# Gate and up products of a hybrid encoder's FFNs as 2x2 block products with seven half-size products

## The chip, the cores and the metric

The kernel runs on one core of a Trainium2 chip. The metric is the device time of one execution in microseconds; lower is better. TensorE multiplies matrices, VectorE (DVE in the profile) and ScalarE (ACT) do element-wise work and read and write PSUM, GpSimd (POOL) helps with element-wise work on SBUF, and SyncE (SP) starts the loads. Each engine runs its own instructions in order and waits on semaphores for the others.

## The reference

Two layers work on 512 tokens of 1024 features in float32. Every layer is a half-step SwiGLU FFN, a mixer (a Conformer convolution in layer 0, a bidirectional HGRN2 recurrence in layer 1) and a second half-step FFN; there are four FFNs in all.

```
def swiglu(h, w13, w2):
    gate, up = jnp.split(h @ w13, 2, axis=-1)
    return (jax.nn.silu(gate) * up) @ w2

for layer in range(DEPTH):
    x = x + FFN_RES * swiglu(rms_norm(x, norm_g[layer, 0]), ffn_w13[layer, 0], ffn_w2[layer, 0])
    h = rms_norm(x, norm_g[layer, 1])
    mix = conformer_conv(...) if layer % 2 == 0 else hgrn2_bidirectional(...)
    x = x + mix
    x = x + FFN_RES * swiglu(rms_norm(x, norm_g[layer, 2]), ffn_w13[layer, 1], ffn_w2[layer, 1])
return rms_norm(x, final_g)
```

The product `h @ w13` takes 1024 features to 2 x 2816 (gate and up); `w2` takes 2816 back to 1024.

## The kernel before

Activations lie with features on the 128 partitions: `xs[k]`, k = 0 to 7, are eight tiles of 128 features by 512 tokens. The norm's gain is applied and each tile is split into a rounded part and a rest, `xh[k]` (cast on ScalarE, L230) and `xl[k]` (VectorE, L231), in the format fp32r. Weights are split in the same way after they are loaded: ScalarE casts `whi` (L124), VectorE subtracts to get `wlo` (L125). A product of full accuracy is then three matmuls:

```
    def mm3(o, wh, wl, ah, al, first, last):
        nc.tensor.matmul(o, lhsT=wh, rhs=ah, start=first, stop=False)
        nc.tensor.matmul(o, lhsT=wh, rhs=al, start=False, stop=False)
        nc.tensor.matmul(o, lhsT=wl, rhs=ah, start=False, stop=last)
```

An FFN (L340) runs in two halves of 11 pairs. A pair j is one tile of 128 gate features and the same tile of up features; each is a `proj` (L306) of 8 k-tiles x 3 matmuls of 512 columns (one column per token), so a pair is 48 matmuls. Its evacuation (L357 to L365) multiplies both by the norm's factor `rs` (L358, L360), takes the SiLU (L362), multiplies (L363) and splits the result into `gh`, `gl` (L364, L365). After the 11 pairs of a half come 8 output tiles o of the down product, 33 matmuls each, added to `xs[o]` (L399). In the second half every finished `xs[o]` is at once prepared for the next phase (`next_prep`, L400 to L401): the split above, and its squares added up on GpSimd (L241).

The RMS norm's factor is not ready when a phase's first products start. `Lead` (L277) puts the small products of the norm between the first groups and holds evacuations back until the factor is there. In an FFN the factor is worked out in every partition at once (`norm_wide`, L258: two matmuls and some ten VectorE instructions of 512 columns); before the convolution and the recurrence it is worked out on 4 columns (`norm_stats_pe`, L243) and spread by four small products (`norm_bc`, L252).

The convolution and the recurrence end with a D-to-D product (`k_outer`): six output tiles are accumulated side by side and finish one after another (six matmuls each at the end), then output tiles 6 and 7 follow with 24 matmuls each, whose weights come from one last chunk in two parts. Each finished tile updates `xs[o]` (L634 or L925) and goes through `next_prep`.

A static scheduler orders each engine's instructions at build time and sets the semaphores; `whi`/`wlo` rotate through three buffers, raw weights through three, and PSUM has six banks for products (tag `mm`) and two for small ones (`aux`).

## Time and profile before

| | |
|---|---|
| time, median of 3 runs | 2073.39 us (2072.43 to 2074.63) |
| profiled execution: span from first to last instruction | 2068.9 us (the page gives no time around it) |
| TensorE busy | 2029.7 us, 98% of the span, 9223 matmuls |
| VectorE busy | 1111.9 us, 54% |
| ScalarE busy | 766.5 us, 37% |
| mean granted TensorE clock | 0.993 of full speed |

The span is 4.5 us below the median of the timed runs. Busy times are the union of an engine's instructions. TensorE's instructions overlap in the records: a matmul is listed with its whole duration, and the next one starts before it is over, so the rate is read from the distance of two starts. PEld is the load of the stationary operand, which each matmul has.

### The profile page before, as it was taken

The page shows a single profiled execution, that of the slowest core. Times are in us where ns is not written, and L with a number is a line of the kernel's source. Part 1 is how long each engine was busy: PE and PEld are TensorE (multiplying, and loading weights), DVE is VectorE, ACT ScalarE, POOL GpSimd, SP SyncE. Part 2 cuts the span into 40 slices and gives each one's busy share as a digit, 9 for nine tenths or more (in the row PEclk, how much of TensorE's full clock was granted, in tenths as well). Part 3 has the DMA queues.
Part 4 walks back from the last instruction along what each step waited for, and adds up shares of the span by engine and source line. Part 5 has one row for each costly group of instructions (what it writes and reads, how often), then busy time and mean ns, then how long its engine had stood idle before and what let it go on. Part 6 is the DMA issues. An engine that isn't in the chain of part 4 may idle for free.

```text
span 2068.9 us, 22882 instructions
## 1 busy us (share of the span) xinstructions
PE 2029.7 (98%) x9223; PEld 1656.7 (80%) x9223; DVE 1111.9 (54%) x1560; ACT 766.5 (37%) x1151; POOL 254.4 (12%) x201
## 2 busy tenths in 40 slices
PE   8999999998899999999999999999999999999997
PEld 6888888765688888888888888888888888888886
DVE  7433444598674434445443444378758865434433
ACT  5322233566343222233222323355545443222332
POOL 2000001399420000010000001111101020000002
PEclk9999999999899999999999999999999999999998
DMA  5223223211122232223223222311111122223221
GB/s 196 96 71 129 90 75 111 82 56 46 57 100 87 84 110 102 83 91 122 84 82 111 101 83 91 121 62 61 62 62 52 51 102 102 77 97 108 90 84 55
DMA packets 32170, 182.49 MB, mean 88 GB/s; under 512 B 3536, under 2 KB 6736, under 8 KB 17088
## 3 DMA queue, kind: packets, MB, share of 16 engines
q1 hardware_dynamic: 31376, 180.04, 25.0%
q8 instruction: 72, 1.18, 0.2%
q10 hardware_dynamic: 544, 0.52, 0.1%
q0 software_dynamic: 144, 0.46, 0.1%
q14 instruction: 34, 0.28, 0.0%
HBM read 178.92 MB, written 2.10 MB: 87 GB/s over the span
## 4 chain that ended last, share of the span: by engine, by line
PE 88%; DVE 6%; POOL 3%; issue 2%; ACT 1%; DMA 0%; SPq 0%; DVEq 0%; POOLq 0%
PE mm L153 27%; PE mm L151 27%; PE mm L152 27%; PE aux L778 2%; POOL ga L507 2%; DVE mm L499 1%; DVE wlo L125 1%; DVE Q L812 1%; PE mm L681 1%; PE mm L683 1%; PE mm L682 1%; PE aux L850 1%; DVE k L813 1%; PE mm L490 1%; PE aux L852 0%
## 5 line engine op out<-in xcount | busy, mean ns | idle before, releaser
L124 ACT CAST whi<-wraw 128x1024 fp32r<-128x1024 f32 (+3 forms) x386 | 362.3, 940 | 990.3 <-PE mm L152 710.5
L151 PE MATMUL mm<-xh,whi 128*128 128x512 f32 x1792 | 710.8, 397 | 7.5 <-ACT whi L124 7.5
L153 PE MATMUL mm<-xh,wlo 128*128 128x512 f32 x1792 | 702.0, 392 | 4.4 <-DVE wlo L125 4.3
L152 PE MATMUL mm<-xl,whi 128*128 128x512 f32 x1792 | 700.1, 391 | 0.9 <-DVE xl L231 0.9
L125 DVE TENSOR_TENSOR wlo<-wraw,whi 128x1024 fp32r<-128x1024 f32 (+3 forms) x386 | 428.5, 1111 | 242.9 <-ACT whi L124 238.7
L153 PEld LDWEIGHTS mm<-xh,wlo 128*128 128x128 f32 x1792 | 337.1, 188 | 78.2 <-DVE wlo L125 8.6
L151 PEld LDWEIGHTS mm<-xh,whi 128*128 128x128 f32 x1792 | 337.5, 188 | 76.9 <-ACT whi L124 7.5
L152 PEld LDWEIGHTS mm<-xl,whi 128*128 128x128 f32 x1792 | 337.5, 188 | 72.2 <-issue 3.4
L151 PE MATMUL mm<-gh,whi 128*128 128x512 f32 (+1 forms) x715 | 279.6, 391 | 0.0
L153 PE MATMUL mm<-gh,wlo 128*128 128x512 f32 (+1 forms) x715 | 278.5, 390 | 0.0
L152 PE MATMUL mm<-gl,whi 128*128 128x512 f32 (+1 forms) x715 | 276.4, 387 | 0.0
L241 POOL TENSOR_TENSOR ss<-ss,sq 128x512 f32<-128x512 f32 x48 | 71.3, 1485 | 1477.0 <-ACT sq L240 1469.9
L360 DVE TENSOR_TENSOR t<-mm,rs 128x512 f32<-128x512 f32 x88 | 60.8, 691 | 267.2 <-PE mm L153 267.2
L153 PEld LDWEIGHTS mm<-gh,wlo 128*128 128x128 f32 x715 | 134.2, 188 | 30.7
L152 PEld LDWEIGHTS mm<-gl,whi 128*128 128x128 f32 x715 | 134.3, 188 | 29.7
L151 PEld LDWEIGHTS mm<-gh,whi 128*128 128x128 f32 x715 | 134.4, 188 | 27.3
L358 DVE TENSOR_TENSOR t<-mm,rs 128x512 f32<-128x512 f32 x88 | 60.8, 691 | 171.7 <-PE mm L153 171.6
L399 DVE SCALAR_TENSOR_TENSOR x<-mm,x 128x512 f32<-128x512 f32 x63 | 43.6, 692 | 124.8 <-PE mm L153 124.8
L507 POOL TENSOR_TENSOR ga<-ga,pr 128x512 f32<-128x512 f32 x67 | 99.4, 1484 | 23.6 <-ACT pr L506 19.9
L364 ACT CAST gh<-t 128x512 fp32r<-128x512 f32 x88 | 54.5, 621 | 71.6 <-DVE t L363 71.6
L499 DVE SCALAR_TENSOR_TENSOR mm<-u,vec,mm 128x512 f32<-128x512 f32 x106 | 74.5, 745 | 4.3 <-PE mm L490 4.0
L778 PEld LDWEIGHTS aux<-Q,kp 128*128 128x128 f32 x448 | 58.5, 191 | 17.7 <-issue 10.0
(209 smaller groups left out, 1621.5 us busy)
## 6 DMA issues: line engine op xcount, KB each, us to landing
wraw<-in_w SPq DMA_DIRECT2D x87, 1024.0 KB, 4.8
wraw<-in_w SPq DMA_DIRECT2D x64, 704.0 KB, 4.1
wraw<-in_win SPq DMA_DIRECT2D x16, 1024.0 KB, 4.8
wraw<-in_pw SPq DMA_DIRECT2D x8, 1024.0 KB, 4.8
wraw<-in_kout SPq DMA_DIRECT2D x8, 768.0 KB, 4.2
wraw<-in_win_i SPq DMA_DIRECT2D x4, 1024.0 KB, 4.8
x<-in_xT SPq DMA_DIRECT2D x8, 256.0 KB, 5.9
wraw<-in_kout SPq DMA_DIRECT2D x2, 1024.0 KB, 4.7
```

Of the source, the lines that this page charges most:

```text
L124: nc.scalar.copy(hi[:, a:b], raw[:, off + a:off + b])
L125: nc.vector.tensor_tensor(lo[:, a:b], raw[:, off + a:off + b], hi[:, a:b].bitcast(F32), op=ALU.subtract)
L151: nc.tensor.matmul(o, lhsT=wh, rhs=ah, start=first, stop=False)
L152: nc.tensor.matmul(o, lhsT=wh, rhs=al, start=False, stop=False)
L153: nc.tensor.matmul(o, lhsT=wl, rhs=ah, start=False, stop=last)
L241: nc.gpsimd.tensor_tensor(norm["ss"], norm["ss"], sq, op=ALU.add)
L358: nc.vector.tensor_tensor(gs, pg, rs(), op=ALU.mult)
L360: nc.vector.tensor_tensor(us, pu, rs(), op=ALU.mult)
L364: nc.scalar.copy(h_, us)
L499: nc.vector.scalar_tensor_tensor(acc, u[:, t:t + S], wcol(j, t), acc, op0=ALU.mult, op1=ALU.add)
L507: nc.gpsimd.tensor_tensor(ga, ga, pr, op=ALU.add)
L778: nc.tensor.matmul(sp[:, c * P:(c + 1) * P], lhsT=kp[:, c * P:(c + 1) * P], rhs=view(Q, hl, c), start=True, stop=True)
```

## The change

The 2x2 block product splits three things in two: the output of a pair (gate tile, up tile), the features summed over (even k-tiles, odd k-tiles; the layout of `w13` puts them in four runs of 512 columns: a11, a12 for gate, a21, a22 for up) and the tokens (left 256, right 256: b11, b12 for even, b21, b22 for odd k-tiles). Instead of eight block products there are seven, of sums and differences of the blocks (Winograd's form of Strassen's product).

- Weights (`seven_w`): per pair VectorE forms four sums of 512 columns (s12 and s43), then four operands are split: wa (s12, 1024 columns), wb (a11 and a12 as loaded, 1024), wc (s43, 1024) and wd (a22, 512). The splits use the lines L129 and L130 now. wa, wb and wc together take all three `whi`/`wlo` buffers; wd has one of its own.
- Activations (`seven_x`): per two k-tiles seven operands of 256 columns (slots 0 to 6 of `x7h`, `x7l`), four of them sums or differences.
- Products (`seven`, `seven_pair`): each of the seven is 4 k-tiles x 3 matmuls of 256 columns, so 84 matmuls a pair. They are accumulated into two PSUM tiles x (gate) and y (up); ScalarE copies partial results (L468, L469, L492, L497), VectorE adds others (both through the helper `add`, L149). The seventh product, of wd, is put into the next pair (`close`). The first pair of a half has another order and a third tile z (L482, L485).
- The first two pairs of the first FFN stay plain products, on the same operand tiles (`plain_pairs`); `seven_x` of all eight tiles comes between them and rewrites slots that the second reads.
- The evacuation no longer multiplies `up` by the norm's factor; the factor, halved (`rs05`), is applied to the down product instead, which then takes two VectorE instructions per output tile (L579 and an add) in place of one.
- The FFNs use the norm on 4 columns too; `norm_wide` is gone. Before the first products six matmuls of ones run.
- The convolution's and the recurrence's `next_prep` is `seven_x` now, as is that between the third and the second FFN.

```
+NP = KD // 2
+T2 = S // 2
...
+PLAIN = 2
...
-                plan.append((w13[f, half * HALF + j], [1024, 1024]))
+                plain = f == 0 and half == 0 and j < PLAIN
+                plan.append((w13[f, half * HALF + j], [1024, 1024] if plain else [2048]))
...
+            if sz > D:
+                ready[i] = seven_w(raws[ci])
+                state["split"] += 1
+                continue
             hi = wp.tile([P, D], F32R, name="whi", tag="whi", bufs=3)
...
+    def seven_w(raw):
+        q = D // 2
+        a11, a12, a21, a22 = (raw[:, i * q:(i + 1) * q] for i in range(4))
+        s12 = st["R"].tile([P, D], F32, name="s12", tag="s12")
+        s43 = st["R"].tile([P, D], F32, name="s43", tag="s43")
+        add(s12[:, :q], a21, a22)
+        add(s12[:, q:], s12[:, :q], a11, ALU.subtract)
+        wa = wtile()
+        split(*wa, s12, 0, 0, D)
+        wb = wtile()
+        split(*wb, raw, 0, 0, D)
+        add(s43[:, :q], a12, s12[:, q:], ALU.subtract)
+        add(s43[:, q:], a11, a21, ALU.subtract)
+        wc = wtile()
+        split(*wc, s43, 0, 0, D)
+        wd = [st["R"].tile([P, q], F32R, name=n, tag=n) for n in ("wdh", "wdl")]
+        split(*wd, raw, 3 * q, 0, q)
+        return wa, wb, wc, wd
...
+    def open_x7():
+        st["R"] = r = operands("x7")
+        for n, l in (("x7h", x7h), ("x7l", x7l)):
+            l[:] = [r.tile([P, 7 * T2], F32R, name=f"{n}{k}", tag=f"{n}{k}") for k in range(NP)]
...
+    for _ in range(6):
+        nc.tensor.matmul(psum(), lhsT=ones_r, rhs=ones_r[:, 0:1].broadcast_to([P, S]), start=True, stop=True)
...
+    def seven_x(k, gc):
+        kp, g = k // 2, col(gc + k)
+        h, l = x7h[kp], x7l[kp]
+        left, right = xs[k][:, :T2], xs[k][:, T2:]
+        def both(a, b, src):
+            nc.scalar.copy(h[:, a * T2:b * T2], src)
+            add(l[:, a * T2:b * T2], src, h[:, a * T2:b * T2].bitcast(F32), ALU.subtract)
+        def less(o, a, b):
+            nc.vector.scalar_tensor_tensor(o, a, g, b, op0=ALU.mult, op1=ALU.subtract)
+        if k % 2 == 0:
+            fa = tp.tile([P, S], F32, name="t0", tag="t0")
+            fb = tp.tile([P, S], F32, name="t1", tag="t1")
+            st["f"] = fa, fb
+            nc.scalar.activation(fb[:, :T2], right, AF.Copy, scale=g)
+            nc.scalar.activation(fa[:, :T2], left, AF.Copy, scale=g)
+            add(fa[:, T2:], fb[:, :T2], fa[:, :T2], ALU.subtract)
+            both(0, 2, fa)
+        else:
+            fa, fb = st["f"]
+            fc = tp.tile([P, S], F32, name="t2", tag="t2")
+            o = slice(2 * T2, 4 * T2)
+            nc.scalar.activation(h[:, o], xs[k], AF.Copy, scale=g)
+            less(l[:, o], xs[k], h[:, o].bitcast(F32))
+            less(fc[:, :T2], right, fb[:, :T2])
+            less(fc[:, T2:], right, fa[:, T2:])
+            both(4, 6, fc)
+            less(fb[:, T2:], left, fc[:, T2:])
+            both(6, 7, fb[:, T2:])
...
+        for n, f in (("rs", 1.0), ("rs05", 0.5)):
+            norm[n] = tp.tile([P, S], F32, name=n, tag=n, bufs=1)
+            nc.scalar.mul(norm[n], b, f)
...
+    def plain_x(k, b12):
+        kp = k // 2
+        if k % 2:
+            o = slice(2 * T2, 4 * T2)
+            return [(slice(0, S), x7h[kp][:, o], x7l[kp][:, o])]
+        o = slice(kp % 2 * T2, (kp % 2 + 1) * T2)
+        return [(slice(0, T2), x7h[kp][:, :T2], x7l[kp][:, :T2]),
+                (slice(T2, S), b12[kp // 2][0][:, o], b12[kp // 2][1][:, o])]
...
+                wnext()
+                for k in range(KD):
+                    seven_x(k, C_NORM)
...
+    def seven(o, w, i, slot, start=False, kps=range(NP)):
+        x = slice(slot * T2, (slot + 1) * T2)
+        for kp in kps:
+            sl = slice((i * NP + kp) * P, (i * NP + kp + 1) * P)
+            for a, b in ((w[0], x7h), (w[0], x7l), (w[1], x7h)):
+                nc.tensor.matmul(o, lhsT=a[:, sl], rhs=b[kp][:, x], start=start and kp == 0 and a is w[0] and b is x7h,
+                                 stop=kp == NP - 1 and a is w[1], skip_group_check=True)
+    def seven_pair(lead, close, done):
+        wa, wb, wc, wd = wget()
+        x, y = psum(), psum()
+        l, r = slice(0, T2), slice(T2, S)
+        cs = st["R"].tile([P, 3 * T2], F32, name="cs", tag="cs")
+        p5, u2, u3 = (cs[:, i * T2:(i + 1) * T2] for i in range(3))
+        def seed():
+            nc.scalar.copy(y[:, l], x[:, l])
+            nc.scalar.copy(p5, x[:, r])
+        if close is None:
+            z = psum()
+            for kps in (range(NP - 1), range(NP - 1, NP)):
+                seven(x[:, r], wa, 0, 1, True, kps)
+                seven(x[:, l], wb, 0, 0, False, kps)
+                if kps[-1] == NP - 1:
+                    seed()
+                seven(z[:, l], wb, 1, 2, True, kps)
+                seven(z[:, r], wc, 0, 3, False, kps)
+            lead.group()
+            zs = tp.tile([P, S], F32, name="t0", tag="t0")
+            nc.scalar.copy(zs, z)
+            add(x, x, zs)
+            seven(y[:, l], wa, 1, 5)
+            nc.scalar.copy(u2, y[:, l])
+        else:
+            seven(x[:, r], wa, 0, 1, True)
+            seven(x[:, l], wb, 0, 0)
+            seed()
+            close()
+            seven(y[:, l], wa, 1, 5)
+            nc.scalar.copy(u2, y[:, l])
+            seven(x[:, l], wb, 1, 2)
+            seven(x[:, r], wc, 0, 3)
+        add(x[:, r], x[:, r], u2)
+        seven(y[:, l], wc, 1, 4)
+        nc.scalar.copy(u3, y[:, l])
+        add(y[:, r], u3, p5)
+        if close is None:
+            lead.group()
         wnext()
-        return pg, pu
-    def ffn(next_prep, first=None, tail=None):
+        def end():
+            seven(y[:, l], wd, 0, 6)
+            if lead.n == 2:
+                lead.group()
+            done(x, y)()
+        return end
...
+                def evac(j, pg, pu):
+                    def f():
+                        gh[j] = h_ = gp.tile([P, S], F32R, name=f"gh{j}", tag=f"gh{j}")
+                        gl[j] = l_ = gp.tile([P, S], F32R, name=f"gl{j}", tag=f"gl{j}")
                         gs = tp.tile([P, S], F32, name="t0", tag="t0")
                         nc.vector.tensor_tensor(gs, pg, rs(), op=ALU.mult)
-                        us = tp.tile([P, S], F32, name="t1", tag="t1")
-                        nc.vector.tensor_tensor(us, pu, rs(), op=ALU.mult)
                         sg = tp.tile([P, S], F32, name="t2", tag="t2")
                         nc.scalar.activation(sg, gs, AF.Silu)
-                        nc.vector.tensor_tensor(us, us, sg, op=ALU.mult)
+                        us = tp.tile([P, S], F32, name="t1", tag="t1")
+                        nc.vector.tensor_tensor(us, pu, sg, op=ALU.mult)
                         nc.scalar.copy(h_, us)
                         nc.vector.tensor_tensor(l_, us, h_.bitcast(F32), op=ALU.subtract)
-                    lead.evac(evac)
+                    return f
...
+                for j in range(HALF):
+                    if first is not None and half == 0 and j < PLAIN:
+                        if j == 0:
+                            first(lead, gp, evac)
+                        continue
+                    close = seven_pair(lead, close, lambda x, y, j=j: evac(j, x, y))
...
+                        if o == 0 and k == 2:
+                            close_last()
                     wnext()
-                    nc.vector.scalar_tensor_tensor(xs[o], p, 0.5, xs[o], op0=ALU.mult, op1=ALU.add)
+                    pn = tp.tile([P, S], F32, name="t0", tag="t0")
+                    nc.vector.tensor_tensor(pn, p, norm["rs05"], op=ALU.mult)
+                    add(xs[o], xs[o], pn)
...
+    ffn(open_x2, prep_for(1), plain_pairs)
+    conv(seven_for(2))
+    ffn(open_x7, seven_for(3))
+    ffn(open_x2, prep_for(4))
+    hgrn(seven_for(5))
...
-    w13 = np.asarray(ffn_w13).reshape(4, KD, P, 2, NFF, P).transpose(0, 4, 2, 3, 1, 5).reshape(4, NFF, P, 2 * D)
+    w13 = np.asarray(ffn_w13).reshape(4, NP, 2, P, 2, NFF, P).transpose(0, 5, 3, 4, 2, 1, 6).reshape(4, NFF, P, 2 * D)
```

The static scheduler orders the new instructions anew. Three places are shown here as they stand in each engine's order; numbers behind names are buffers.

On VectorE, a pair in the middle of the first FFN's second half; `mm` are the two PSUM tiles of a pair, t0 to t2 the evacuation's temporaries. Before:

```order
L125 TENSOR_TENSOR wlo_1734<-wraw_1595,whi_1733 128x1024
L360 TENSOR_TENSOR t1_1701<-mm_1668,rs_285 128x512
L363 TENSOR_TENSOR t1_1701<-t1_1701,t2_1703 128x512
L125 TENSOR_TENSOR wlo_1765<-wraw_1666,whi_1764 128x1024
L365 TENSOR_TENSOR gl4_1698<-t1_1701,gh4_1697 128x512
L358 TENSOR_TENSOR t0_1770<-mm_1708,rs_285 128x512
```

After, the same place; s12 and s43 are the sums of the weights, cs holds ScalarE's copies, `mm_2781` is x and `mm_2782` is y of the pair:

```order
L130 TENSOR_TENSOR wlo_2893<-wraw_2652,whi_2892 128x1024
L149 TENSOR_TENSOR mm_2781<-mm_2781,cs_2783 128x256
L149 TENSOR_TENSOR s12_3011<-s12_3011,wraw_2779 128x512
L523 TENSOR_TENSOR t0_2951<-mm_2781,rs_466 128x512
L149 TENSOR_TENSOR mm_2782<-cs_2783 128x256
L130 TENSOR_TENSOR wlo_2899<-s43_2885,whi_2898 128x1024
L149 TENSOR_TENSOR s43_3012<-wraw_2779,s12_3011 128x512
L149 TENSOR_TENSOR s43_3012<-wraw_2779 128x512
L527 TENSOR_TENSOR t1_2955<-mm_2782,t2_2953 128x512
L130 TENSOR_TENSOR wdl_2903<-wraw_2652,wdh_2902 128x512
L529 TENSOR_TENSOR gl6_2950<-t1_2955,gh6_2949 128x512
L130 TENSOR_TENSOR wlo_3016<-s12_3011,whi_3015 128x1024
```

Six instructions a pair became thirteen (the thirteenth, the first sum s12 of the pair after next, follows the last row), with the parts of three pairs' weights between the two sums into PSUM and the evacuation.

On ScalarE, the start of the second half of the first FFN, where the casts of the down product's weights end. Before:

```order
L124 CAST whi_1327<-wraw_1241 128x640
L124 CAST whi_1348<-wraw_1286 128x1024
L124 CAST whi_1378<-wraw_1286 128x1024
L124 CAST whi_1409<-wraw_1331 128x1024
L124 CAST whi_1449<-wraw_1331 128x1024
```

After; `mm_2037` is the first pair's x, `mm_2038` its y and `mm_2040` its z, `whi_2126` and `whi_2130` are wa and wb of the second pair, and the last row is the copy u2:

```order
L129 CAST whi_2024<-s43_2011 128x1024
L468 COPY mm_2038<-mm_2037 128x256
L469 COPY cs_2039<-mm_2037 128x256
L129 CAST whi_2126<-s12_2122 128x1024
L482 COPY t0_2091<-mm_2040 128x512
L129 CAST whi_2130<-wraw_1993 128x1024
L485 COPY cs_2039<-mm_2038 128x256
```

Between the copy of the first sum and u2 stand two casts of the next pair's weights; the first of them needs the buffer that the first pair's wa leaves.

On VectorE, the end of the convolution, where output tiles 4 and 5 of `k_outer` are added to x4 and x5 and the last split of `k_outer`'s own weights (for output tile 7) comes. Before:

```order
L634 SCALAR_TENSOR_TENSOR x4_74<-mm_3830,vec_94,x4_74 128x512
L231 SCALAR_TENSOR_TENSOR xl3_89<-x3_73,vec_94,xh3_81 128x512
L634 SCALAR_TENSOR_TENSOR x5_75<-mm_3831,vec_94,x5_75 128x512
L125 TENSOR_TENSOR wlo_4077<-wraw_3946,whi_4076 128x1024
L231 SCALAR_TENSOR_TENSOR xl4_90<-x4_74,vec_94,xh4_82 128x512
```

After:

```order
L818 SCALAR_TENSOR_TENSOR x4_74<-mm_5168,vec_89,x4_74 128x512
L305 SCALAR_TENSOR_TENSOR t1_5362<-x3_73,vec_89,t2_5378 128x256
L149 TENSOR_TENSOR x7l1_5066<-t2_5378,x7h1_5062 128x512
L818 SCALAR_TENSOR_TENSOR x5_75<-mm_5169,vec_89,x5_75 128x512
L149 TENSOR_TENSOR x7l1_5066<-t1_5362,x7h1_5062 128x256
L149 TENSOR_TENSOR t0_5398<-t1_5399,t0_5398 128x256
L305 SCALAR_TENSOR_TENSOR t2_5415<-x5_75,vec_89,t1_5399 128x256
L305 SCALAR_TENSOR_TENSOR x7l2_5067<-x5_75,vec_89,x7h2_5063 128x512
L149 TENSOR_TENSOR x7l2_5067<-t0_5398,x7h2_5063 128x512
L305 SCALAR_TENSOR_TENSOR t2_5415<-x5_75,vec_89,t0_5398 128x256
L130 TENSOR_TENSOR wlo_5454<-wraw_5284,whi_5453 128x1024
```

Before, that split came right after the update of x5; now nearly all of the third `seven_x` (x4 with x5) and the rest of the second stand ahead of it, 21 instructions of `seven_x` since the update of x0 against four splits `xl` before.

## Rows read from the trace of the kernel before

**Rows 1.** The page: the span, and part 1, busy time, share and instructions by engine.

```profile
span 2068.9 us, 22882 instructions
...
PE 2029.7 (98%) x9223; PEld 1656.7 (80%) x9223; DVE 1111.9 (54%) x1560; ACT 766.5 (37%) x1151; POOL 254.4 (12%) x201
```

**Rows 2.** Windows: a stretch of FFN pairs; busy us by engine, PEclk, DMA share, GB/s.

```profile
60.00:160.00 100.00, 100.00 (x442) 82.61 (x441) 42.28 (x52) 26.86 (x34) 0.00 (x0) 1.00 0.24 82
```

**Rows 3.** Timeline, last output tile in token halves: start, us, instruction [idle before <-releaser].

```profile
2044.52 0.28 PE L151 MATMUL mm<-gh,whi 128*128 128x256 f32 x1
2044.53 0.19 PEld L152 LDWEIGHTS mm<-gl,whi 128*128 128x128 f32 x1
...
2044.64 0.19 PEld L153 LDWEIGHTS mm<-gh,wlo 128*128 128x128 f32 x1
...
2048.32 0.28 PE L153 MATMUL mm<-gh,wlo 128*128 128x256 f32 x1
```

**Rows 4.** Lines by form: count, busy us and mean ns, idle before and releaser.

```profile
L241 POOL TENSOR_TENSOR ss<-ss,sq 128x512 f32<-128x512 f32 x48 | 71.3, 1485 | 1477.0 <-ACT sq L240 1469.9 <-DVE wlo L125 6.2
...
L363 DVE TENSOR_TENSOR t<-t,t 128x512 f32<-128x512 f32 x88 | 60.6, 690 | 6.6
...
L364 ACT CAST gh<-t 128x512 fp32r<-128x512 f32 x88 | 54.5, 621 | 71.6 <-DVE t L363 71.6
```

**Rows 5.** Timeline, the end of the kernel: instructions of 256 columns.

```profile
2048.64 0.42 DVE L960 SCALAR_TENSOR_TENSOR x<-mm,x 128x256 f32<-128x256 f32 x1 [3.22 <-PE mm L153]
...
2054.30 0.37 ACT L978 COPY rows<-aux 128x256 f32<-128x256 f32 x1 [4.39 <-PE aux L218]
```

**Rows 6.** Timeline, an FFN pair: what follows a matmul or a cast.

```profile
100.41 0.39 PE L153 MATMUL mm<-xh,wlo 128*128 128x512 f32 x1
...
100.84 0.69 DVE L360 TENSOR_TENSOR t<-mm,rs 128x512 f32<-128x512 f32 x1 [3.30 <-PE mm L153]
...
106.11 1.05 ACT L124 CAST whi<-wraw 128x1024 fp32r<-128x1024 f32 x1 [3.12 <-PE mm L152]
...
107.19 1.22 DVE L125 TENSOR_TENSOR wlo<-wraw,whi 128x1024 fp32r<-128x1024 f32 x1 [0.22 <-ACT whi L124]
```

**Rows 7.** Timeline, VectorE at the end of the convolution.

```profile
570.04 1.55 DVE L634 SCALAR_TENSOR_TENSOR x<-mm,vec,x 128x512 f32<-128x512 f32 x2
...
575.94 1.13 DVE L231 SCALAR_TENSOR_TENSOR xl<-x,vec,xh 128x512 fp32r<-128x512 f32 x1
...
577.65 1.66 DVE L125 TENSOR_TENSOR wlo<-wraw,whi 128x1024 fp32r<-128x1024 f32 x1
...
582.64 1.21 DVE L125 TENSOR_TENSOR wlo<-wraw,whi 128x1024 fp32r<-128x1024 f32 x1
583.77 0.74 DVE L634 SCALAR_TENSOR_TENSOR x<-mm,vec,x 128x512 f32<-128x512 f32 x1
```

**Rows 8.** Timeline, GpSimd in the same stretch.

```profile
573.27 8.89 POOL L241 TENSOR_TENSOR ss<-ss,sq 128x512 f32<-128x512 f32 x5 [28.33 <-ACT sq L240]
```

**Rows 9.** Timeline, the start: last split of the activations, start of the third pair.

```profile
20.90 1.76 DVE L231 SCALAR_TENSOR_TENSOR xl<-x,vec,xh 128x512 fp32r<-128x512 f32 x1
...
35.36 0.39 PE L151 MATMUL mm<-xh,whi 128*128 128x512 f32 x1
```

**Rows 10.** Timeline, TensorE: output tile 7 of the convolution, first and last matmul.

```profile
581.78 0.39 PE L151 MATMUL mm<-yh,whi 128*128 128x512 f32 x1
...
587.12 0.39 PE L153 MATMUL mm<-yh,wlo 128*128 128x512 f32 x1
```

**Rows 11.** Timeline, end of the recurrence: first update, first matmul of output tile 7.

```profile
1673.29 1.89 DVE L925 TENSOR_TENSOR x<-mm,x 128x512 f32<-128x512 f32 x3 [0.91 <-PE mm L153]
...
1683.62 0.39 PE L151 MATMUL mm<-onh,whi 128*128 128x512 f32 x1
```

**Rows 12.** Timeline, the end: two small dependent VectorE instructions.

```profile
2052.49 0.16 DVE L203 TENSOR_TENSOR fu<-fu,ft 128x2 f32<-128x2 f32 x1
...
2052.68 0.16 DVE L204 SCALAR_TENSOR_TENSOR rf<-fu,rf 128x2 f32<-128x2 f32 x1
```

More of the change, by code (lines that the diff above doesn't have):

```diff
@@ L137, in wsplit, with add, wtile @@
             state["split"] += 1
+    def add(o, a, b, op=ALU.add):
+        nc.vector.tensor_tensor(o, a, b, op=op)
+    def wtile():
+        return [wp.tile([P, D], F32R, name=n, tag=n, bufs=3) for n in ("whi", "wlo")]
+    def seven_w(raw):
[16 more added lines that the diff above has]
+        return wa, wb, wc, wd
     def wget():
@@ L183, in tile_encoder @@
     make_identity(nc, ident)
-    ones = cst.tile([P, P], F32, name="ones")
-    nc.gpsimd.memset(ones, 1.0)
-    ones_r = cst.tile([P, P], F32R, name="ones_r")
-    nc.scalar.copy(ones_r, ones)
     def col(c):
@@ new lines, in tile_encoder, with open_final @@
+    ffn(open_x2, prep_for(1), plain_pairs)
[3 more added lines that the diff above has]
+    hgrn(seven_for(5))
+    fin = {}
+    def open_final():
+        fin["fp"] = fp = operands("fp")
+        fin["yt"] = fp.tile([P, KD, S], F32, name="yt")
+        fin["m"] = fp.tile([P, 4], F32, name="mf")
+        fin["r"] = fp.tile([P, 4], F32, name="rf")
+        fin["last"] = fp.tile([P, S], F32, name="last")
+        fin["rows"] = fp.tile([P, S // 2], F32, name="rows")
@@ new lines, in ys, with prep_final, tail, close @@
+    def ys(k, sl=slice(0, S)):
+        return fin["yt"][:, k, sl]
+    def prep_final(o):
+        norm_sq(o)
+        nc.scalar.activation(ys(o), xs[o], AF.Copy, scale=col(C_FINAL + o))
+    def tail(p, half):
+        sl = slice(half * S // 2, (half + 1) * S // 2)
+        cs = slice(2 * half, 2 * half + 2)
+        o = KD - 1
+        b = []
+        m, r, last, rows, yt = (fin[n] for n in ("m", "r", "last", "rows", "yt"))
+        def close():
+            pn = tp.tile([P, S], F32, name="t0", tag="t0")
+            nc.vector.tensor_tensor(pn[:, sl], p[:, sl], norm["rs05"][:, sl], op=ALU.mult)
+            add(xs[o][:, sl], xs[o][:, sl], pn[:, sl])
+            nc.scalar.activation(last[:, sl], xs[o][:, sl], AF.Square)
+            nc.scalar.activation(ys(o, sl), xs[o][:, sl], AF.Copy, scale=col(C_FINAL + o))
+            if half == 0:
+                a = psum("aux")
+                token_sum(norm["ss"], a)
+                nc.vector.tensor_scalar(m, a[:, 0:4], 1.0 / D, EPS, op0=ALU.mult, op1=ALU.add)
+        def measure():
+            a = psum("aux")
+            token_sum(last, a, 0, range(2 * half, 2 * half + 2))
+            nc.vector.scalar_tensor_tensor(m[:, cs], a[:, cs], 1.0 / D, m[:, cs], op0=ALU.mult, op1=ALU.add)
+            rsqrt(r[:, cs], m[:, cs], *(fin["fp"].tile([P, 2], dt, name=n, tag=n)
+                                        for n, dt in (("fg", I32), ("ft", F32), ("fu", F32))))
+        def spread():
+            b.append(bcast(r, range(2 * half, 2 * half + 2)))
+            if half == 0:
+                nc.scalar.copy(rows, b[0][:, sl])
+        def scale():
+            for k in range(KD):
+                if half == 0:
+                    nc.gpsimd.tensor_tensor(ys(k, sl), rows, ys(k, sl), op=ALU.mult)
+                else:
+                    nc.vector.tensor_tensor(ys(k, sl), b[0][:, sl], ys(k, sl), op=ALU.mult)
+                if k % 2:
+                    e = nc.scalar if half and k % 4 == 3 else nc.sync
+                    e.dma_start(out[k - 1:k + 1, :, sl].rearrange("k p t -> p k t"), yt[:, k - 1:k + 1, sl])
+        return close, measure, spread, scale
```

214 lines of the change are left out of this document (96 added, 118 removed).

## The prediction, as put on record before the changed kernel ran

> **What bounds the kernel now.** I read the page's busy shares first: TensorE is busy for 98% of the span, VectorE 54%, ScalarE 37% [rows 1]. Since a share is a mean over stages, I next took a window inside the first FFN, where the change is: there TensorE is never idle, VectorE is busy 42% and ScalarE 27%, DMA engines 24%, at the full granted clock [rows 2]. It issues 442 matmuls in 100 us, one of 512 columns every 0.2262 us; the listed duration is longer, because matmuls overlap, so I use the distance of starts. A pair of 48 costs 48 x 0.2262 = 10.86 us. So in the FFNs only the number and width of matmuls counts, as long as nobody makes TensorE wait. Then I read the places where a phase ends and the next begins, where VectorE has its queue [rows 7 to 12].
>
> **The steady saving.** Products of 256 columns occur once in the trace before, in the last output tile. From the first to the last of one half are 32 distances in 2048.32 - 2044.52 = 3.80 us, 0.1188 each [rows 3]; twice that is 0.2375, 5% above a 512-column one. A new pair is 84 x 0.1188 = 9.98 us. It saves 0.88 us, far less than an eighth of 10.86 (1.36), since 256-column products pay that 5%. There are 4 x 22 pairs less 2 plain ones: 86 x 0.88 = **-76 us**. The two plain pairs compute half of their k-tiles in halves: 2 x 24 x 0.0113 = **+0.5**.
>
> One rule speaks against this, and can be left out of the sum: the Trainium skill, "TensorE: Matmul & The Clock Gate", section "The mechanism", says that a weight load overlaps matmuls in flight only when it goes to another row group, which these loads of all 128 rows do not. A load lasts 0.19 us, yet two loads start 0.11 apart between 256-column matmuls [rows 3], so the trace disagrees: by the rule a pair would be 84 x 0.19 = 16.0 us, by the rows 9.98.
>
> **Do the other engines keep up in a pair?** VectorE had six instructions a pair: two splits of 1024 columns (1.22, [rows 6]) and four of 512 (0.69, [rows 4]), 5.2 us. Now there are thirteen: three splits of 1024, eight of 512 columns (four sums, wdl, three of the evacuation) and two adds of 256 (0.42, [rows 5]): 3.66 + 5.52 + 0.84 = 10.02 us, as a sum of durations more than the pair has. But independent instructions start 0.08 before the end of the one ahead (582.64 + 1.21 against 583.77, [rows 7]); 13 x 0.08 taken off leaves 8.98, 90% of 9.98. ScalarE: three casts (1.05, [rows 6]), three of 0.62 [rows 4], four copies of 256 (0.37, [rows 5]): 6.5. It is no bound.
> I laid the order of VectorE against the slots of the seven products (each 12 x 0.1188 = 1.43). The tightest place is y: its copy u3 ends at about 11.6 us after the pair's start, the add into y's right half runs from 11.64 to 12.06, and TensorE's product of wd in the same bank is due at 12.83; wlo of wa ends 8.2 against 10.2, wlo of wb 10.0 against 11.6. All slack is 0.6 us or more and VectorE's cycle closes with 1.0 us to spare, so I cost the added VectorE work in steady pairs at nothing; what hides it is TensorE's 9.98. Without that cover see the first rival.
>
> **What the edges cost.** Here the trace shows the pieces, not the wait, so each has two ends.
> *The start, +14 (6 to 22).* The last split of the activations ends at 22.66 and the third pair starts at 35.36 [rows 9]. Now all of `seven_x` has to run before the third pair. Per two tiles it is 3 VectorE instructions of 512 and 5 of 256 columns, 3 x 0.61 + 5 x 0.34 = 3.5 with overlap, 14 for eight tiles, and 1.2 for a split among them: from about 25.3, where the norm's first small work is done, to 41. The second plain pair reads slots that `seven_x` rewrites and its up weights stand behind it, so it ends near 45.8, 10.4 later than 35.36. In the first seven-product pair come wlo of wa 0.7, the factor 0.7 and the evacuation chain ahead of u2, about 2. Low end: `seven_x` runs under the two plain pairs (21.7 us of TensorE), and only 6 are left; high end: the two do not overlap at all after the first pair.
> *Second halves, 4 x 2.4 = +9.6 (1.0 to 3.3 each).* The copy u2 stands behind a cast that needs wa's buffer, free at 7.1 us; with zs (0.62) and a second cast (1.05) u2 ends at 10.4 instead of 8.0, and wc's second product, which rewrites y, waits 3.3, less 0.8 of later products that the order puts ahead.
> *Convolution to FFN, +12 (4 to 16).* From the first x update at 570.04 [rows 7] VectorE has, up to the last split of the weights, six updates (4.0), the 21 instructions of `seven_x` (8 of 512 and 13 of 256 columns: 9.8), and that split (1.1). GpSimd's five square sums run there from 573.27 for 8.89 us [rows 8], and beside them instructions of 512 columns took 1.13 instead of 0.74 and splits 1.66 instead of 1.21 [rows 7], about half more; I add 3.8, and 0.8 for dependent instructions, which start 0.10 after what they need (the 0.16 us ones follow at 0.19, [rows 12]; the subtraction starts 0.03 after its cast, [rows 6]). That is 589.5. TensorE starts output tile 7 at 581.78 and is through it by 587.3, six matmuls in the last stretch [rows 10]; it needs wlo at about 582.7, so it waits 7. Then u2 1.3, wlo of wa 0.6, the norm's factor (its instructions of 4 columns stand between `seven_x`'s) 2.3 and the small products 0.9. Low end: the split is early enough and only the second group is left.
> *Recurrence to FFN, +10 (4 to 16).* The same queue from 1673.29, output tile 7 at 1683.62 [rows 11]: wlo at about 1689.3, 5 late, and 5 for the rest.
> *FFN to FFN, +4.5 (1 to 7).* No D-to-D product, so only u2 1.2, the factor 2.5, small products 0.8. The tail: the extra VectorE instruction of the last output tile and later u copies, +0.6. The six matmuls of ones cost nothing: the first pair waits for VectorE's splits (22.66, [rows 9]).
> A second rule bears on the phase ends: the Trainium skill, "SBUF — State Buffer", section "SBUF: two separate sides", calls the port that VectorE and GpSimd share an exclusive lock for a whole instruction. One addition of GpSimd lasts 1.49 [rows 4], but VectorE's instructions beside it grew by 0.4 [rows 7], so the trace shows less than that; with a whole addition's wait for each of five, a phase end would cost 5 x 1.49 - 3.8 = 3.6 us more, an estimate inside my ranges.
>
> Sum: -76 + 0.5 + 14 + 9.6 + 12 + 10 + 4.5 + 0.6 = -25. Span 2068.9 - 25 = 2044; the median of the timed runs is 4.5 above the span of before, so **2048 us**, the likeliest's own range 2022 to 2068 (the ends of the edges taken mostly independently).
>
> **Rivals.**
> *VectorE becomes the bound of a pair.* One mechanism: if thirteen instructions do not overlap by 0.08 (four need what the one ahead writes, others wait for ScalarE) the cycle is 10.02 plus four waits of 0.1 to 0.15, 10.5 us; TensorE then loses 0.52 in each of 78 steady pairs, +41, and the time is 2089, slower. It decides against before from a cycle of 10.3 on (25 / 78 above 9.98). For it: the sum of durations exceeds the slot. Against: the overlap stands in rows 7, and ScalarE has 3.5 us free per pair. 17%.
> *The edges are nearly hidden.* The scheduler has put the split and u2 late in the order, but if VectorE gets through faster (no wait between instructions, GpSimd beside other work), only some 10 of the 51 us are lost: 2007. Against it: at the start TensorE can not overlap with work that its operands need. 12%.
> *256-column products do not keep 0.119.* Rows 3 are one place with weights prepared long before; if a weight load (0.19) had to stand alone, a pair is 16 us and the time 2073 + 86 x 5.1, about 2510. Rows 3 show 33 in a row without it. 2%.
>
> **How the numbers follow.** The main case has 69%. A measurement here tells 0.2% from no change, 4.1 us: faster is below 2069.2, slower above 2077.5. Faster: 66 of the 69, and the 12 of the second rival, with 1 of the first: 0.79. Same: 0.04, from the edges' upper ends. Slower: 0.17. The range of 8 in 10 runs from the second rival's 2006 to the first one's 2090.
>
> **What would show it.** Starts of 256-column matmuls in FFN pairs 0.119 apart, TensorE still without gaps in steady windows, VectorE near 90% busy there. The third pair starts near 46. At the ends of the convolution and recurrence TensorE waits for wlo of output tile 7 (L130), at the half starts for the copy u2. If steady windows show TensorE waiting for VectorE (the add into y first), the first rival holds, and the forecast is wrong; if the waits at the edges sum to under 20 us, the second.

## The result, and the profile after

The changed kernel takes 2041.72 us (median of 4 runs, 2041.40 to 2041.82) against 2073.90 before: ratio 0.9848, 95% interval 0.9834 to 0.9862. The forecast was 2048; the profiled span is 2039.9 us against 2068.9 [rows 1]. The medians differ by 32.2 us, the spans by 29.0. Nearly all timed runs whose span is on record lie 1.8 us above it, so by estimate the profiled execution of before took 2070.7, some 3 us under its median; what follows compares one execution each.

The page after, span and part 1, in the columns of [rows 1]:

```profile
span 2039.9 us, 30786 instructions
...
PE 1977.2 (97%) x12429; PEld 1754.4 (86%) x12429; DVE 1554.6 (76%) x2337; ACT 1046.2 (51%) x1757; POOL 253.7 (12%) x201
```

TensorE issues 3206 matmuls more in 52 us less of busy time; VectorE has 443 us more work. The window inside the second half of the first FFN, in the columns of [rows 2], and four starts of wd's product, one pair apart, on the timeline:

```profile
215.00:305.00 90.00, 89.94 (x764) 89.72 (x763) 83.01 (x117) 55.18 (x92) 0.00 (x0) 1.00 0.29 99
```

```profile
242.94 0.29 PE L455 MATMUL mm<-x7h,wdh 128*128 128x256 f32 x1
...
252.82 0.29 PE L455 MATMUL mm<-x7h,wdh 128*128 128x256 f32 x1
...
262.71 0.29 PE L455 MATMUL mm<-x7h,wdh 128*128 128x256 f32 x1
...
272.60 0.29 PE L455 MATMUL mm<-x7h,wdh 128*128 128x256 f32 x1
```

A pair takes (272.60 - 242.94) / 3 = 9.89 us, a matmul 0.1177. TensorE stands still for 0.06 us of the 90, and VectorE is busy 92%. Before, the eleven pairs of the same half ran from the first matmul of the first pair to the first of the down product:

```profile
193.72 0.40 PE L151 MATMUL mm<-xh,whi 128*128 128x512 f32 x1
...
313.45 0.40 PE L151 MATMUL mm<-gh,whi 128*128 128x512 f32 x1
```

That is 119.73 us, 10.88 a pair. What waits after the change, the profile's list of TensorE's waits says (who waits for whom, us in total, how often, the longest):

```profile
PE mm L189 <- DVE wlo L130: 10.5, 6, 5.4
...
PE mm L455 <- ACT whi L129: 4.8, 3, 4.2
...
PE aux L271 <- POOL ss L334: 4.0, 1, 4.0
PE mm L455 <- DVE wlo L130: 3.5, 6, 0.9
```

8.0 us of the first are output tile 7 of the two D-to-D products; the second is the casts of the next FFN's wa and wb, the third the last sum of squares at the start. The end of the convolution, TensorE, answers to [rows 10]:

```profile
586.55 0.38 PE L455 MATMUL mm<-x7h,whi 128*128 128x256 f32 x1 [4.18 <-ACT whi L129]
586.77 0.36 PE L455 MATMUL mm<-x7l,whi 128*128 128x256 f32 x1
589.71 0.80 PE L189 MATMUL mm<-yh,wlo 128*128 128x512 f32 x1 [2.58 <-DVE wlo L130]
590.30 0.63 PE L187 MATMUL mm<-yh,whi 128*128 128x512 f32 x1
590.73 0.63 PE L188 MATMUL mm<-yl,whi 128*128 128x512 f32 x1
```

It waits 4.2 us for a cast of the next FFN's first pair, some of whose matmuls the schedule has put ahead of output tile 7, then 2.6 us for that tile's split, and is then slow: starts are 0.43 apart where [rows 10] have 0.23. The windows of the slow stretch and of the 2 us behind it show why, in PEclk:

```profile
589.71:593.69 3.98, 3.98 (x10) 3.13 (x10) 3.98 (x7) 2.38 (x5) 0.78 (x1) 0.50 0.72 257
594.00:596.00 2.00, 2.00 (x10) 1.61 (x9) 0.85 (x2) 0.00 (x0) 2.00 (x1) 1.00 0.40 66
```

The granted clock is at its lower level, 1.2 of 2.4 GHz, behind the wait. The same follows the 5.4 us wait at the recurrence's end (0.53 from 1668.48 to 1672.50), and the 4.0 us wait at the start (0.50 from 25 to 30).

Where the 29 us come from: each stretch ends with the start of a phase's last matmul; a pair saves 10.88 - 9.89 = 1.0 us, and what is missing from that is the edge.

| stretch | before | after | difference | saving of its pairs | edge |
|---|---|---|---|---|---|
| start to end of FFN 1, first half | 193.49 | 200.53 | +7.0 | 9.0 | 16.0 |
| second halves of FFN 1, 2, 3, each | 180.17 | 170.52 | -9.65 | 11.0 | 1.3 |
| second half of FFN 4 | 183.78 | 173.42 | -10.4 | 11.0 | 0.6 |
| convolution and first half of FFN 2 | 394.06 | 398.64 | +4.6 | 11.0 | 15.6 |
| first half of FFN 3 | 180.65 | 173.98 | -6.7 | 11.0 | 4.3 |
| recurrence and first half of FFN 4 | 561.96 | 566.95 | +5.0 | 11.0 | 16.0 |

### The profile page after: what moved, and what is told of

The parts are those of the page before. It is cut to its first block, busy times and chain, and to the rows that moved or that the text cites. A ratio compares the mean times of both kernels' runs of the same rounds, so it can differ in the third digit from the quotient of the medians.

```text
span 2039.9 us, 30786 instructions
## 1 busy us (share of the span) xinstructions
PE 1977.2 (97%) x12429; PEld 1754.4 (86%) x12429; DVE 1554.6 (76%) x2337; ACT 1046.2 (51%) x1757; POOL 253.7 (12%) x201
## 4 chain that ended last, share of the span: by engine, by line
PE 82%; DVE 9%; POOL 4%; issue 2%; ACT 2%; DMA 0%; SPq 0%; DVEq 0%; POOLq 0%; ACTq 0%
PE mm L455 39%; PE mm L187 11%; PE mm L189 11%; PE mm L188 11%; PE aux L963 3%; POOL ga L689 3%; DVE wlo L130 2%; DVE mm L681 1%; DVE t L305 1%; DVE x7l L149 1%; PE mm L868 1%; PE mm L866 1%; PE mm L867 1%; PE aux L1035 1%; DVE x7l L305 1%
## 5 line engine op out<-in xcount | busy, mean ns | idle before, releaser
L455 PE MATMUL mm<-x7h,whi 128*128 128x256 f32 x2064 | 578.5, 281 | 8.5 <-ACT whi L129 4.8
L455 PE MATMUL mm<-x7h,wlo 128*128 128x256 f32 x2064 | 577.9, 280 | 3.6 <-DVE wlo L130 3.5
L455 PE MATMUL mm<-x7l,whi 128*128 128x256 f32 x2064 | 577.5, 280 | 0.0
L130 DVE TENSOR_TENSOR wlo<-wraw,whi 128x1024 fp32r<-128x1024 f32 (+2 forms) x292 | 319.0, 1092 | 147.5 <-ACT whi L129 142.9
L129 ACT CAST whi<-wraw 128x1024 fp32r<-128x1024 f32 (+2 forms) x292 | 268.7, 921 | 314.0 <-PE mm L188 282.0
L455 PEld LDWEIGHTS mm<-x7h,whi 128*128 128x128 f32 x2064 | 388.0, 188 | 11.5 <-ACT whi L129 6.3
L455 PEld LDWEIGHTS mm<-x7h,wlo 128*128 128x128 f32 x2064 | 387.8, 188 | 5.3 <-DVE wlo L130 5.2
L455 PEld LDWEIGHTS mm<-x7l,whi 128*128 128x128 f32 x2064 | 388.1, 188 | 0.3
L129 ACT CAST whi<-s 128x1024 fp32r<-128x1024 f32 x172 | 180.5, 1049 | 163.6 <-PE mm L455 119.7
L130 DVE TENSOR_TENSOR wlo<-s,whi 128x1024 fp32r<-128x1024 f32 x172 | 210.1, 1221 | 33.6 <-ACT whi L129 32.4
L187 PE MATMUL mm<-xh,whi 128*128 128x512 f32 x384 | 163.1, 425 | 0.0
L189 PE MATMUL mm<-xh,wlo 128*128 128x512 f32 x384 | 154.7, 404 | 2.5 <-DVE wlo L130 2.5
L188 PE MATMUL mm<-xl,whi 128*128 128x512 f32 x384 | 153.1, 399 | 0.0
L579 DVE TENSOR_TENSOR t<-mm,rs 128x512 f32<-128x512 f32 x63 | 43.5, 690 | 108.4 <-PE mm L189 108.4
L149 DVE TENSOR_TENSOR s<-wraw 128x512 f32<-128x512 f32 x172 | 117.4, 686 | 6.6 <-DMA wraw<-in_w 4.7
```

The costliest lines, as they stand in the source:

```text
L129: nc.scalar.copy(hi[:, a:b], raw[:, off + a:off + b])
L130: nc.vector.tensor_tensor(lo[:, a:b], raw[:, off + a:off + b], hi[:, a:b].bitcast(F32), op=ALU.subtract)
L149: nc.vector.tensor_tensor(o, a, b, op=op)
L455: nc.tensor.matmul(o, lhsT=a[:, sl], rhs=b[kp][:, x], start=start and kp == 0 and a is w[0] and b is x7h, stop=kp == NP - 1 and a is w[1], ...
L579: nc.vector.tensor_tensor(pn, p, norm["rs05"], op=ALU.mult)
```

## The experiments

The times are medians of four runs; the ratio is against the kernel before on the same chip. Differences against the changed kernel are those of profiled spans (2039.9 us) or of stretches of the table, one execution each; where that matters, the difference of the ratios stands beside it.

| run | time, us | ratio to before, 95% interval | span, us |
|---|---|---|---|
| changed kernel | 2041.72 | 0.9848 (0.9834 to 0.9862) | 2039.9 |
| e1_ends | 2040.38 | 0.9845 (0.9831 to 0.9860) | 2037.3 |
| e2_ve1 | 2047.25 | 0.9881 (0.9866 to 0.9896) | 2043.3 |
| e3_ve2 | 2053.56 | 0.9907 (0.9890 to 0.9923) | 2053.5 |
| e4_short | 1971.64 | 0.9515 (0.9500 to 0.9529) | 1968.4 |
| e5_nogps | 2019.99 | 0.9748 (0.9734 to 0.9763) | 2015.7 |
| e6_head | 2035.22 | 0.9824 (0.9809 to 0.9838) | 2034.7 |
| e7_nowarm | 2042.95 | 0.9860 (0.9845 to 0.9875) | 2041.3 |
| e8_both | 2033.05 | 0.9811 (0.9794 to 0.9827) | 2031.7 |
| e9_fill | 2042.28 | 0.9851 (0.9836 to 0.9866) | 2041.3 |
| e10_vsum | 2028.88 | 0.9787 (0.9770 to 0.9803) | 2027.0 |
| e11_tsum | 2018.91 | 0.9738 (0.9724 to 0.9753) | 2016.4 |

**Who bounds a pair.** Three runs load VectorE or relieve TensorE.

```
         add(s43[:, q:], a11, a21, ALU.subtract)
+        add(s43[:, q:], a11, a21, ALU.subtract)     # e2_ve1: once more; e3_ve2: twice
...
-    def seven(o, w, i, slot, start=False, kps=range(NP)):      # e4_short
+    def seven(o, w, i, slot, start=False, kps=range(NP - 1)):
...
```

> The changed kernel with one more VectorE instruction of 512 columns per seven-product pair (the last sum of s43 computed twice, 0.60 us). Theory (TensorE's 9.89 us set a pair, VectorE has 9.05 of work in it): 9.65 still fits, 0 to +8 us. Rival (VectorE is already the bound, the rest of its time is waiting it can't avoid): 86 x 0.60 = +52 us.

> The changed kernel with two more VectorE instructions of 512 columns per pair (the last sum of s43 computed three times, 1.20 us). Theory: VectorE's 10.25 us now set a pair, 0.36 above TensorE's 9.89: +25 to +45 us. If TensorE still covered it (slack larger than its idle share): below +10. Rival (VectorE was the bound before): +103 us.

> The changed kernel with a quarter of the gate and up products left out (each of the seven sums over three of its four k-tiles, 63 matmuls a pair instead of 84); VectorE's and ScalarE's work is whole. Theory: TensorE would need 7.42 us a pair, so the pair's time is then VectorE's own cycle, 9.05 of work and some waits, 9.1 to 9.5 us: -35 to -70 us, VectorE busy 95% or more in the pairs. Rival (VectorE has much more room than its busy share says, and TensorE alone sets the pair): 86 x 2.47 = -212 us.

The same stretch of pairs in windows, e3_ve2 and then e4_short:

```profile
215.00:305.00 90.00, 89.94 (x762) 89.57 (x761) 89.46 (x133) 52.91 (x91) 0.00 (x0) 1.00 0.29 99
```

```profile
206.00:290.00 84.00, 71.96 (x570) 68.29 (x569) 81.62 (x118) 53.63 (x91) 0.00 (x0) 1.00 0.31 106
```

The split wdl, once a pair on VectorE, in e4_short:

```profile
214.34 0.68 DVE L130 TENSOR_TENSOR wdl<-wraw,wdh 128x512 fp32r<-128x512 f32 x1
...
288.45 0.69 DVE L130 TENSOR_TENSOR wdl<-wraw,wdh 128x512 fp32r<-128x512 f32 x1
```

With a quarter of the matmuls gone a pair takes 9.26 us (eight pairs between these two starts), VectorE is busy 97% and TensorE waits: the saving is 71 us, not 212. So VectorE's own cycle is 9.26, 0.63 under TensorE's 9.89; the forecast's 8.98 was 0.3 short. One more instruction (e2_ve1) costs 3.4 us of span, within the theory's 0 to 8. Two more fill VectorE to 99% and lengthen its cycle to about 10.1, yet the span grows by 13.6 us only and a second half by 0.25; the 25 us expected were a miss. One reason shows in the trace: VectorE prepares the first pairs' weights during the down product, and this lead is eaten up slowly. In the second half of the first FFN wdl starts 7.6 us ahead of its product at first and 5.8 at last, while in the changed kernel it stays at 7.6 until the last pair. It isn't the whole account: e2_ve1 adds 0.57 us to a second half, more than e3_ve2, and the scheduler orders each kernel anew. Both rivals (VectorE the bound, or far from it) fall.

**The ends of convolution and recurrence.**

```
...
+                wsplit(state["use"] + 2)            # behind the updates of x0 to x5
+                for o in range(EARLY, NOUT):        # EARLY = 2
+                    prep(o)
...
```

> The changed kernel, with one thing moved: at the ends of the convolution and of the recurrence the split of the weights of output tile 7 is issued right after the update of x5, and seven_x of tiles 2 to 5 after it. Theory (VectorE's queue at the phase ends sets TensorE's wait, which also costs TensorE half its clock for some 4 us behind it): the waits for wlo L130 (2.6 and 5.4 us) and most of the 4.2 us wait for a cast go, the stretches at the lower clock with them; at each end 5 to 8 us, in all -10 to -16 us against the changed kernel, 2026 to 2032 us. Rival (the same VectorE work has to be done before the first pair, so the wait only moves behind output tile 7): 0 to -3 us, 2039 to 2042.

The theory falls. The wait for output tile 7 does go, and with it the slow stretch: the convolution gets 9.6 us shorter, the recurrence 8.1. But the FFNs behind them get 7.8 and 7.1 us longer, and the time can't be told from the changed kernel's (2.6 us of span, intervals of the ratio overlap): the rival. TensorE's waits in e1_ends:

```profile
PE mm L456 <- ACT whi L130: 9.4, 4, 8.0
PE mm L456 <- DVE wlo L131: 7.3, 7, 4.1
```

What counts is how much VectorE and ScalarE have to do until the first pair is fed, not the order. So the next run takes work away: it leaves out GpSimd's sums of squares.

```
-            nc.gpsimd.tensor_tensor(norm["ss"], norm["ss"], sq, op=ALU.add)
```

> The changed kernel without GpSimd's sums of squares (the norm's sum is then that of tile 0 alone; ScalarE's squares stay). Theory (beside GpSimd's additions VectorE's instructions of two SBUF operands take about half more, 3.8 us of the wait at the end of the convolution, as much at the end of the recurrence, and the start waits 4.0 us for the last sum): -8 to -16 us. Rival (the addition holds VectorE out for its whole 1.46 us, so a phase end wins five to seven of them): -20 to -35 us. Rival (GpSimd's share is hidden, the queue alone counts): 0 to -4, the start's wait.

The span falls by 24.2 us (its profiled execution was the fastest of four; by the ratios 21), over the theory's 16 and within the first rival's range. By stretch: 8.6 at the start, 8.3 around the convolution's end, 6.0 around the recurrence's, 1.1 at FFN 3. The rows of the changed kernel show the mechanism, GpSimd and then VectorE at the convolution's end:

```profile
584.02 1.48 POOL L334 TENSOR_TENSOR ss<-ss,sq 128x512 f32<-128x512 f32 x1 [4.58 <-ACT sq L333]
585.70 1.27 POOL L334 TENSOR_TENSOR ss<-ss,sq 128x512 f32<-128x512 f32 x1 [0.20 <-ACT sq L333]
592.91 3.09 POOL L334 TENSOR_TENSOR ss<-ss,sq 128x512 f32<-128x512 f32 x1 [5.94 <-ACT sq L333]
```

```profile
584.30 1.49 DVE L305 SCALAR_TENSOR_TENSOR t<-x,vec,t 128x256 f32<-128x256 f32 x1
585.72 1.80 DVE L305 SCALAR_TENSOR_TENSOR x7l<-x,vec,x7h 128x512 fp32r<-128x512 f32 x1
...
588.04 0.47 DVE L305 SCALAR_TENSOR_TENSOR t<-x,vec,t 128x256 f32<-128x256 f32 x1
588.44 1.21 DVE L130 TENSOR_TENSOR wlo<-wraw,whi 128x1024 fp32r<-128x1024 f32 x1
```

An instruction of 0.47 us that starts inside an addition takes 1.49, one of 0.74 takes 1.80: each is held about a us, until the addition is nearly over or past. In e5_nogps the longest instructions of line L305 take 0.49 us (256 columns) and 0.75 (512). It goes the other way too: the addition at 592.91 starts while VectorE is inside an instruction, takes 3.09 us, and VectorE's three instructions beside it keep their time (0.41, 1.21 and 0.68 us). Here the trace agrees with the Trainium skill, "SBUF — State Buffer", section "SBUF: two separate sides" (the shared port as a lock for the whole instruction). The trace before shows it as well, in a row that [rows 7] leave out, two instructions of 0.74 us that took 3.48:

```profile
579.23 3.48 DVE L231 SCALAR_TENSOR_TENSOR xl<-x,vec,xh 128x512 fp32r<-128x512 f32 x2
```

The split of [rows 9], at 1.76 us, is another. After the change the excess of such rows up to 588.4 sums to 4.5 us, near the forecast's 3.8. Another 1.0 falls on the addition at 599.08, and 0.8 of the 8.3 us lies ahead of the D-to-D product; the remaining 2 are not broken down. They are not the clock: TensorE still waits 1.0 and 0.5 us there in e5_nogps, and the granted clock is again 0.50 for 3 us (576.5 to 579.5).

**The clock behind a wait.**

```
+            if o == KD - 1:
+                fill = psum("aux")
+                for _ in range(24):
+                    nc.tensor.matmul(fill, lhsT=ones_r, rhs=ones_r[:, 0:1].broadcast_to([P, S]), start=True, stop=True)
```

> The changed kernel with 24 matmuls of ones (512 columns, 5.4 us, into a bank of their own) ahead of output tile 7 of the convolution and of the recurrence, where TensorE waits 7 and 5.4 us. In the changed kernel ten and nine matmuls behind these waits start 0.43 apart instead of 0.23, 1.9 us a time. Theory (TensorE's clock falls because it stood still): the matmuls fit into the waits and the stretches at half the rate go, -1.5 to -2 us at each of the two places, -3 to -4 in all. Rival (the slow stretch has another cause, such as the tile just written or VectorE's and GpSimd's accesses): the 0.43 stay, and the time is the same or up to 5 us longer.

At the recurrence all 24 stand in the wait, and 0.75 us of it is left. At the convolution the scheduler put 20 ahead of the first matmul of the D-to-D product, 40 us too early, and 4 ahead of output tile 7; 3.5 and 2.7 us of waiting are left. So one place is filled and the other is a control. Windows behind the wait, convolution first:

```profile
589.75:595.30 5.55, 5.55 (x13) 4.39 (x14) 5.14 (x8) 2.46 (x5) 2.34 (x1) 0.51 0.53 192
1669.40:1673.40 4.00, 4.00 (x17) 3.31 (x18) 4.00 (x6) 0.87 (x2) 1.08 (x1) 1.00 0.70 244
```

Where TensorE was kept busy it is at 2.4 GHz, where it waited at 1.2. The recurrence gets 1.7 us shorter, and the FFN behind it 2.2 longer: again the pair's operands are late. The stretch of the convolution gets 1.7 longer, with the 20 matmuls in it, and the time is the same. The cause is shown, its gain is hidden.

**The start.**

```
-            both(0, 2, fa)
+            both(0, 2, fa) if fresh else both(1, 2, fa[:, T2:])
...
+            if fresh:                               # slots 2 and 3; not in the first FFN
```

> The changed kernel; in the first FFN seven_x does not write slots 0, 2 and 3 of x7h and x7l again, where the first plain pair has put the same values. Theory (the head's 15 us are the second plain pair's wait for seven_x, whose slots it reads): it no longer waits, VectorE is rid of 3.5 us, the third pair starts near 38 instead of 48.7: -8 to -12 us, 2030 to 2034. Rival (VectorE must finish all of seven_x before the third pair anyway, only its length counts): -3 to -4 us.

> The changed kernel without the six matmuls of ones at the start. Theory (the first pair waits for VectorE's splits, and TensorE's clock has fallen again in the waits before 20 us): within 1 us of the changed kernel. Rival (they lift the clock for the first pair): +2 to +5 us.

In e6_head the third pair starts at 40.53, 8.2 us earlier, but the next 84 matmuls take 13.8 us instead of 12.3, so the stretch wins 6.6: the theory's mechanism, with less than its 8 to 12. The span wins 5.2, since the stretch of the convolution gets 1.2 longer. There, in the middle of the convolution, a wait has grown from 0.6 to 4.6 us, in e6_head and then in the changed kernel:

```profile
529.05 1.20 PE L278 MATMUL aux<-ident,r 128*128 128x128 f32 x4 [4.57 <-DVE r L267]
```

```profile
533.48 0.77 PE L278 MATMUL aux<-ident,r 128*128 128x128 f32 x2 [0.61 <-DVE r L267]
```

It waits for the factor of the convolution's own norm. In e6_head GpSimd's additions v (from 525.19) come ahead of the last three of VectorE's instructions of 4 columns for it, and these took 1.2 us each instead of 0.16; in the changed kernel they come behind. So one more place was held by GpSimd, by an order that the edit did not aim at. The six matmuls of ones make no difference that shows: the ratio intervals overlap, and the stretch of the start, where they stand, is 0.2 us longer without them. This speaks for the theory, though the times alone could not tell its 1 us from the rival's 2.

**Put together.** e8_both has the edits of e1_ends and e6_head; e10_vsum and e11_tsum move the squares' sum off GpSimd besides (e11_tsum for three of the FFNs).

```
-            nc.gpsimd.tensor_tensor(norm["ss"], norm["ss"], sq, op=ALU.add)
+            add(norm["ss"], norm["ss"], sq)          # e10_vsum
...
+        sq = tp.tile([P, S], F32R, name="sq", tag="sq", bufs=2)          # e11_tsum
+        nc.scalar.activation(sq, xs[k], AF.Square)
+        for c in range(4):
+            nc.tensor.matmul(norm["sum"][:, 2 * c:2 * c + 2], lhsT=sq[:, c * P:(c + 1) * P], rhs=ones_r[:, 0:2], ...
```

> The changed kernel with both edits: the split of output tile 7 ahead of seven_x of tiles 2 to 5 at the two phase ends, and seven_x of the first FFN without the slots that hold the values already. Theory: the two gains are at different places and add up, -18 to -28 us, 2014 to 2024 us. Rival (one of them only moves its wait): -8 to -14.

> The kernel with both edits, and the squares summed by VectorE instead of GpSimd (seven additions a norm, 0.6 us each; none in GpSimd). Theory (GpSimd's additions cost 22 us, by slowing VectorE at the phase ends and by a last sum that comes late): VectorE takes 4.3 us more at each of four places where it is waited for but loses the slowing, 1 to 3 us gained at each: -3 to -12 against the version with both edits, 2021 to 2030 us. Rival (the sums themselves are the cost, wherever they are made): +5 or more.

> The kernel with both edits, and the squares before the first, second and fourth FFN summed on TensorE: ScalarE writes the square in fp32r, four matmuls of 2 columns a tile add it up in a PSUM bank, in place of GpSimd's additions. Theory (GpSimd's additions cost 21 of the 22 us at these three places; 32 small matmuls of about 0.1 us each take 3 us of TensorE where it mostly waits anyway): -10 to -18 us against the version with both edits, 2015 to 2023 us. Rival (TensorE, in order, now waits for each square, and passes the wait on): -5 to +5.

e8_both gains 8.2 us of span, hardly more than e6_head's 5.2 and e1_ends' 2.6 together: the rival, since the ends only move their wait. VectorE makes the sums 4.7 us cheaper than GpSimd, within the theory's 3 to 12 (the intervals of the two ratios still overlap a little), although it is the engine in demand. On TensorE they gain 15.3, within 10 to 18: 8.1 at the recurrence and the FFN behind it, 5.1 at the convolution, 1.9 at the start. Of the 5.1, 2.2 lie ahead of the D-to-D product, where e8_both has the 4.6 us wait of e6_head and e11_tsum has 0.6; that is the order again, and not where the squares are summed. The granted clock around the convolution's end is 1.00 again, against 0.89 after the change and in e8_both, as the windows of e11_tsum and of the changed kernel show:

```profile
570.00:600.00 30.00, 29.69 (x206) 27.30 (x205) 29.00 (x58) 20.04 (x37) 0.00 (x0) 1.00 0.22 76
```

```profile
570.00:600.00 30.00, 23.24 (x107) 19.07 (x106) 27.80 (x40) 19.53 (x34) 11.03 (x7) 0.89 0.20 71
```

e11_tsum, at 2018.91 us, beats both kernels: 2.6% under before, 1.1% under the changed one.

## Why the prediction was right, and where it was off

- **The saving of a pair** was right in kind and 13% small: 1.0 us and not 0.88, -86 in all and not -76. The term that was mis-sized is the matmul's distance: 0.1177 in long runs of pairs against 0.1188 in [rows 3], and 0.2268 for 512 columns (a half of 528 in 119.73 us) against 0.2262. Loads of 0.19 us stood beside matmuls 0.118 apart throughout the steady pairs. So the sentence of the Trainium skill that the prediction set against this ("TensorE: Matmul & The Clock Gate", section "The mechanism": loads overlap matmuls only in another row group) does not hold here; the same section also lets a load into the background weight buffer go ahead, which the prediction did not weigh.
- **TensorE stays the bound** was right; VectorE's cycle is 9.26 and not 8.98. VectorE's share of 92% was expected as 90%.
- **The second halves** cost 1.3 and not 2.4. The step that failed is "the copy u2 stands behind a cast that needs wa's buffer, free at 7.1 us", and so does the sentence on that buffer in the section on the change. ScalarE, at the start of the second half (200.76):

```profile
206.42 1.06 ACT L129 CAST whi<-s 128x1024 fp32r<-128x1024 f32 x1
207.37 0.60 ACT L482 COPY t<-mm 128x512 f32<-128x512 f32 x1
207.90 1.05 ACT L129 CAST whi<-wraw 128x1024 fp32r<-128x1024 f32 x1
208.85 0.37 ACT L485 COPY cs<-mm 128x256 f32<-128x256 f32 x1
```

  The cast starts at 5.7 us with no wait, while wa's last matmul starts at 207.70. So it writes another buffer, wb's by the order of products (its last one ends about then). u2 ends 8.5 us after the start and not 10.4; the wait that is left is 0.6 us, for wlo of the next pair.
- **The convolution's end**: the split of output tile 7 ends at 589.65, forecast 589.5, and TensorE waits 4.2 + 2.6 there, forecast 7. What lacked is the lower clock behind the wait, 2.0 us, and the whole edge is 15.6 (forecast 12). The price of GpSimd's additions was near (4.5 against 3.8) for a wrong reason: VectorE's instructions beside them are not half longer, they are held about 1 us each. The 0.10 for dependent instructions is 0.03 in its rows ([rows 12]); with the 0.08 that independent ones overlap, the 0.11 that its term prices. **The recurrence's end**: TensorE waits 5.4, forecast 5, and the edge is 16.0 against 10, at the upper end of its range. The 5 is partly luck: 1689.3 is 16.0 us behind the first update, where the same queue at the convolution is 19.5, so GpSimd's 3.8 are not in it. Measured are 16.7, with 4.0 for GpSimd's additions but 17 instructions of `seven_x` ahead of the split in place of 21. Behind the D-to-D products 3.6 and 5.7 us are lost, forecast 5.1 and 5. Ahead of them lie 1.7 and 2.4 us that the forecast does not have; the extra VectorE instruction of the last down tile is about half a us of it (an estimate from its 0.68 us), the rest is open.
- **The start** costs 16, forecast 14.5 (14, and 0.5 for the plain pairs' half-width products): the third pair starts at 48.7, forecast 45.8, since the last sum of squares comes from GpSimd at 25.7 and its small products keep VectorE from seven_x until 27.6, not 25.3. FFN 3 costs 4.3, forecast 4.5.
- The sum: -86 + 57 = -29 against -76 + 51 = -25 (57 is the 56.4 of the table's edges and 0.4 behind the last product). The two errors of 10 and 6 have opposite signs, and within the edges the second halves' 5 too many stand against nearly 10 too few at the two mixers, so it is luck that the total is closer than its terms. The forecast time has 4.5 us more than its span, measured are 1.8; these 2.7 and the 4 of the sum are the 6 us by which 2048 was too high.
- Of the rivals, VectorE as the bound did not come about, but is only 0.63 us per pair away; "the edges are nearly hidden" fell; the loads do overlap.
